# Forty mixer blocks with one 512-column product for the high weights, their halves added on eviction, and five modulation blocks placed earlier

## The chip, the core and the metric

The kernel runs on one core of one Trainium2 chip. The metric is the device time of one execution in microseconds (us). The core's engines run beside each other and meet through semaphores: TensorE (PE in the profile, with PEld for its weight loads), VectorE (DVE), ScalarE (ACT), GpSimd (POOL) and SyncE (SP), whose queue issues the large loads. Products land in PSUM; everything else lies in SBUF.

## What is computed

One decoder layer on 256 tokens of width 1024, in float32. The part that the change touches is the token mixer, and the condition vector that scales it:

```python
mod = jax.nn.silu(c) @ mod_w[l] + mod_b[l]
sh1, sc1, g1, sh2, sc2, g2 = jnp.split(mod, 6, axis=-1)
h = rmsnorm(x, norm1_g[l]) * (1.0 + sc1[:, None]) + sh1[:, None]
z = h @ w_in                      # q, k, v, g_dn, r, conv_b, conv_c, conv_h, gate_a, gate_c
...                               # chunked linear attention gives o
y_gla = o @ w_gla_out
conv_out = causal_short_conv(conv_c * conv_h, conv_w)
y_conv = (conv_b * conv_out) @ w_conv_out
y = jax.nn.sigmoid(gate_a) * y_gla + jax.nn.sigmoid(gate_c) * y_conv
x = x + g1[:, None] * (y @ w_out)
...                               # then a mixture of 64 experts and a final norm
```

## The kernel before

**Blocks.** The mixer's weights are 88 blocks of 128 x 1024 floats (512 KB). Blocks 0 to 15 alternate between v and q/k. Then come groups of eight blocks, each block 128 output features: c (16 to 23), r (24 to 31), h (32 to 39), b (40 to 47), a (48 to 55), g (56 to 63), A (64 to 71, `w_gla_out`), C (72 to 79, `w_conv_out`), O (80 to 87, `w_out`). A group's two halves are named c0 and c1, and so on; i counts the four blocks of a half.

**Split precision.** Each weight block is split into a high part (`split_h`, ACT, L340) and a low part (`split_l`, DVE, L347), both of type float32r, into one of three `sp` tiles that hold two blocks each. The activations are split in the same way. `mm_blk` (L356) does three products for each of eight k: high weights by high activations, high weights by low activations, low weights by high activations. All three are 128 x 128 weights by 256 columns and add up in one PSUM half bank.

**PSUM.** Two consecutive blocks, a pair, share one z bank of 512 floats. There are four z banks, taken in turn by `zt()`, so a bank is used again four pairs, that is eight blocks, later. The first product into a bank waits until the engine that read its last contents is done.

**The loop.** One pass for each block b writes, into the engines' in-order queues: the work marked "first", `split_h` of block b+5, the eviction of the block before (`evac`), the work marked "pre", `split_l` of block b+5, the other work due at b, and then block b's products. An eviction does nothing for the first block of a pair; for the second it works on 512 columns. For c it is an ACT copy (`c_evac`, L710), for h a DVE multiply (L763), for b a DVE multiply four blocks later (`b_evac`, L726), for A and C DVE multiplies and adds, for a and g an ACT sigmoid.

**Modulation.** The 48 blocks of `mod_w` come through the same ring of 12 load buffers as the weights. Each is one DVE multiply with a sum (`mod_blk`, L257). 16 are done beside blocks 0 to 15; the table `MODS` names the block beside which each of the other 32 is done. When `mod_blk` or `split_l` is done with a ring buffer, SP issues the next load into it.

**Other work that is named below.** The gates of the linear attention (L453, L463 and L464 on ACT, L449 to L456 on DVE); `k_evac` (L719, L720), the masks of the attention (L498, DVE) and the state products behind them (L506, PE); the reciprocal of the attention's norm (L549, DVE) and the products that spread it (`gla_ss4`, L556, PE, before block 39); `o_norm` (L561, L563); `conv_taps` (L587); the splits of the activations (`put_h` and `put_l`, one line each for all uses, L567 and L570). After the last C block, O0 takes `yhl`, whose last quarter is split just before; its products are written so that k 0 to 5 of two blocks come ahead of k 6 and 7. `st.free` gives a large buffer to the stream of expert weights: tile T9 at block 80 is one (L107). Behind the mixer come the router and 8 groups of experts, whose weights are loaded in 2 MB units.

Of the kernel before, what the change touches and what calls it, by code (L numbers as in the profile page):

```python
# [17 lines left out]
KT = 8  # L18
# [13 lines left out]
FAR = 8192.0  # L32
START = (2, 2, 0, 2, 8)
XS = 38
MODS = (16, 17, 18, 19, 22, 26, 27, 28, 31, 33, 34, 35, 37, 39, 41, 43, 45, 47, 49, 51, 52, 53, 54, 55, 56, 57, 58,
        59, 60, 61, 62, 63)
LA = 5
SPLIT = ("T6", "T7", "T3")
EPS = 1e-6
# [78 lines left out]
def trunk_kernel(ctx: ExitStack, tc: tile.TileContext, xT: bass.AP, c: bass.AP, modw: bass.AP,  # L118
# [4 lines left out]
    V, S, T, G = nc.vector, nc.scalar, nc.tensor, nc.gpsimd  # L123
# [11 lines left out]
    def mt(*shape):  # L135
        i = mring[rot["m"] % len(mring)]
        rot["m"] += 1
        return pm.tile([128, *(shape or (512,))], F32, name="m", tag=f"M{i}")

    def zt(*shape):  # L140
        i = rot["z"] % 4
        rot["z"] += 1
        return pz.tile([128, *(shape or (2, TOK))], F32, name="z", tag=f"Z{i}")
# [16 lines left out]
    mod_at = {}  # L160
    for n, b in enumerate(MODS):
        mod_at.setdefault(b, []).append((4 + n // 4, n % 4))
    blocks = []
    for j in range(len(items) + LA):
        if j < len(items):
            kind, n, i = items[j]
# [38 lines left out]
    gt2 = sm.tile([128, 1024], F32, name="gt")  # L205
# [62 lines left out]
    A1 = sm.tile([128, KT], F32, name="A1")  # L268
    hhl = big.tile([128, 2, KT, TOK], F32R, name="hhl", tag="T4")
    hl = (hhl[:, 0], hhl[:, 1])  # L270
# [23 lines left out]
    for i in range(2):  # L294
        ps = mt()
# [11 lines left out]
    ps = mt(2, 256)  # L307
    for k in (0, 1, 4, 5):
        if k % 4 == 0:
            start_warm(1 + k // 4)  # L310
        for tt in range(TT):
            T.matmul(ps[:, tt, 0:1], xnt[:, k, 128 * tt:128 * tt + 128], onec, start=(k == 0 and tt == 0),  # L312
                     stop=(k == 5), skip_group_check=True)
# [15 lines left out]
    def sp_slot(b):  # L329
        p = b // 2  # L330
        return p % 3 if p <= XS else (p - XS - 1) % 2

    def sp(b):
        return spt[sp_slot(b)][:, b % 2]

    def split_h(b):
        if b >= len(items):
            return
        kind, n, i = items[b]
        S.copy(sp(b)[:, 0], st.block("w", n, i))  # L340

    def split_l(b):
        if b >= len(items):
            return
        kind, n, i = items[b]
        t = sp(b)
        V.tensor_sub(t[:, 1], st.block("w", n, i), t[:, 0].bitcast(F32))  # L347
        st.bdone("w", n, i)
# [3 lines left out]
    def mm_blk(b, ps, rhs, k0=0, k1=KT, clear=True):  # L352
        t = sp(b).rearrange("p s (k m) -> p s k m", k=KT)
        for k in range(k0, k1):
            for n, (ws, rs) in enumerate(PASSES):
                T.matmul(ps, t[:, ws, k], rhs[rs][:, k], start=(clear and k == 0 and n == 0),  # L356
                         stop=(k == KT - 1 and n == 2), skip_group_check=True)

    def mm_qk(b, kk):
        t = sp(b).rearrange("p s (h m) -> p s h m", h=2 * H)  # L360
        for n, (ws, rs) in enumerate(PASSES):
            for h in range(2 * H):
                pb = (pq, pk)[h // H][h % H // 2]
                T.matmul(pb[:, h % 2], t[:, ws, h], hl[rs][:, kk],  # L364
                         start=(kk == 0 and h % 2 == 0 and n == 0),
                         stop=(kk == KT - 1 and h % 2 == 1 and n == 2), skip_group_check=True)

    def mm_v(b, kk, pv):
        t = sp(b)
        for n, (ws, rs) in enumerate(PASSES):  # L370
            for tt in range(TT):
                for hh in range(2):
                    T.matmul(pv[tt][hh], hl[rs][:, kk, 128 * tt:128 * tt + 128],  # L373
                             t[:, ws, 512 * hh:512 * hh + 512],
                             start=(kk == 0 and n == 0), stop=(kk == 7 and n == 2))

    def prep(b):

        k = b // 2
        split_h(b)  # L380
        if b % 2 == 0:
            if k > 0:
                mods(k)
            h_mod(k)
            if k > 0:
                split_l(b - 1)
                if k < KT - 1:
                    xnorm(k + 1)
            h_lo(k)
            split_l(b)  # L390
            if k == 0:
                S.copy(rstd1, pr1[:, :TOK])
                xnorm(1)
# [9 lines left out]
    L = {}  # L403
# [162 lines left out]
    def put_h(dst, x, s):  # L566
        S.copy(dst[:, 0, s], x)  # L567

    def put_l(dst, x, s):
        V.tensor_sub(dst[:, 1, s], x, dst[:, 0, s].bitcast(F32))  # L570
# [22 lines left out]
    def at(i, f, *a):  # L593
        todo.setdefault(i, []).append((f, a))
# [4 lines left out]
    def pre(i, f, *a):  # L599
        todo.setdefault((i, "pre"), []).append((f, a))  # L600
# [71 lines left out]
    def x1_out(k, ps):  # L672
        V.scalar_tensor_tensor(xres[:, k], ps, modc[:, 16 + k:17 + k], xres[:, k], op0=OP.mult, op1=OP.add)
# [31 lines left out]
    ps = None  # L705
# [37 lines left out]
    def r_evac(q, ps):  # L743
        S.activation(L["sr"][:, 2 * q:2 * q + 2], ps, AF.Silu)

    def evac(b, kind, n, i, ps):
        if kind in ("v", "qk"):
            return
        if n == "O1" and i >= 2:
            x1_out(4 + i, ps[i - 2][:, 0])  # L750
            at(b + 1, x1_stat, 4 + i)
            return
        half = int(n[1:])
        q = 2 * half + i // 2
        s = slice(2 * q, 2 * q + 2)
        if i % 2 == 0:
            return
        if kind == "r":
            pre(b, r_evac, q, ps)
        elif kind == "c":  # L760
            pre(b, c_evac, s, ps)
        elif kind == "h":
            V.tensor_mul(cu0[:, s], cu0[:, s], ps)  # L763
            at(b + 1, conv_tap0, s)
            at(b + 2, conv_taps, s)
        elif kind == "b":
            pre(b + 4, b_evac, q, ps)
            at(b + 5, b_high, q)
            at(b + 6, b_low, q)
        elif kind in "ag":  # L770
            if kind == "a" and q == 0:
                L["sg"] = big.tile([128, 2, KT, TOK], F32, name="sg", tag="T8")
            S.activation(L["sg"][:, 0 if kind == "a" else 1, s], ps, AF.Sigmoid)
        elif kind == "A":
            V.tensor_mul(L["sg"][:, 0, s], L["sg"][:, 0, s], ps)
            if q == 3:
                st.free("T11")
        elif kind == "C":
            if q == 0:
                L["yhl"] = big.tile([128, 2, KT, TOK], F32R, name="yhl", tag="T4")  # L780
            y, t = L["sg"][:, 0, s], L["sg"][:, 1, s]
            V.tensor_mul(t, t, ps)
            V.tensor_add(y, y, t)
            put_h(L["yhl"], y, s)
            if q < 3:
                at(b + 1, put_l, L["yhl"], y, s)
            else:
                put_l(L["yhl"], y, s)
                at(b, st.free, "T9")
                at(b + 2, o_setup)  # L790
        elif kind == "O":
            for k in range(2 * q, 2 * q + 2):
                x1_out(k, ps[:, k % 2])
            at(b + 1, x1_stats, q)
# [9 lines left out]
    def run(b):  # L804
        for f, a in todo.pop(b, []):
            f(*a)
# [8 lines left out]
            ahead.setdefault(b - (LA if b // 2 <= XS + 2 else LA - 2), []).append(b)  # L815
    for b, (kind, n, i) in enumerate(items):
        if i % 2 == 0 and kind not in ("v", "qk"):
            ps = (zt(), zt()) if n == "O1" and i == 2 else zt()
        nxts = ahead.get(b, ())
        early = b + LA < nb and items[b + LA][0] in ("v", "qk")  # L820
        run((b, "first"))
        if early:
            prep(b + LA)
        for nxt in nxts:
            if items[nxt - 1][0] == "qk":
                split_l(nxt - 1)
            split_h(nxt)
        if pend:
            evac(b, *pend)
        run((b, "pre"))  # L830
        for nxt in nxts:
            split_l(nxt)
        run(b)
        if kind == "v":
            mm_v(b, b // 2, pv)
        elif kind == "qk":
            mm_qk(b, b // 2)
        else:
            rhs = {"A": "ohl", "C": "chl", "O": "yhl"}.get(kind)
            rhs = hl if rhs is None else (L[rhs][:, 0], L[rhs][:, 1])  # L840
            if n == "O0" and i == 0:
                mm_blk(b, ps[:, 0], rhs, 0, 6)
                mm_blk(b + 1, ps[:, 1], rhs, 0, 6, clear=False)
                mm_blk(b, ps[:, 0], rhs, 6, 8)
            elif n == "O0" and i == 1:
                mm_blk(b, ps[:, 1], rhs, 6, 8)
            elif n == "O1" and i >= 2:
                mm_blk(b, ps[i - 2][:, 0], rhs)
            else:
                mm_blk(b, ps[:, i % 2], rhs)  # L850
        pend = (kind, n, i, ps)
        if b % 2 and all(sp_slot(a) != sp_slot(b) for a in range(b + 1, nb)):
            st.free(SPLIT[sp_slot(b)])
# [30 lines left out]
    O1, O2 = OO[:, :, 0], OO[:, :, 1]  # L884
# [264 lines left out]
    for g in range(NGRP):  # L1149
# [6 lines left out]
        ps = pa.tile([128, D], F32, name="a")  # L1156
# [21 lines left out]
        ps = pa.tile([128, D], F32, name="a")  # L1178
# [137 lines left out]
```

## Time and profile before

| | |
|---|---|
| time, median of 3 runs | 1210.06 us (1209.81 to 1211.35) |
| the profiled execution | 1211.79 us, span of its trace 1210.0 us |
| mean granted TensorE clock | 0.885; 1.00 in every 20 us stretch from 0 to 320 us |
| busy share: PE, PEld, DVE, ACT | 75%, 40%, 31%, 19% |
| HBM traffic | 477.84 MB, 394 GB/s over the span |

The times of the sections below are those of the profiled execution, in us from the start of its span. The busy shares are means over two very different parts: the mixer up to about 296 us, and the experts behind it. In the timeline rows, a row merges instructions of one line that follow each other, so its length is that of all of them, and the first number in brackets is the idle time of the engine ahead of it, with what ended it.

### The profile page before, as it was taken

The numbers are of one execution on the slowest core, as the hardware profiler recorded it, in microseconds if no ns is written. First come the engines' busy times: TensorE is split into PE (matmuls) and PEld (weight loads), VectorE is DVE, ScalarE is ACT, GpSimd is POOL, SyncE is SP. The second block draws the span as 40 slices with busy tenths as digits, with TensorE's granted clock in tenths as the row PEclk, the third lists the DMA queues.
The fourth block names the chain that finished last, engine by engine and source line by source line (L and its number), as shares of the span: only waits on it lengthen the run. The fifth ranks groups of instructions, "written<-read, shape, count | busy, mean of one in ns | idle before, by whom it ended". The sixth has DMA issues, their size and how long they took to land.

```text
span 1210.0 us, 14630 instructions
## 1 busy us (share of the span) xinstructions
PE 912.2 (75%) x6202; PEld 478.8 (40%) x6202; DVE 380.1 (31%) x718; ACT 224.7 (19%) x375; POOL 4.0 (0%) x15
## 2 busy tenths in 40 slices
PE   9999999999887667766666767565667666757565
PEld 6999999999341212121212122121212111312112
DVE  8967699654430202111111111020202000302103
ACT  6774545343310101010101010000000000100002
POOL 0000000000000000000000000000000000000000
PEclk9999999999997978788888788898878787988787
DMA  9997579979999999999999999999999999999995
GB/s 368 394 342 246 183 233 346 368 277 358 413 430 431 430 431 430 432 429 431 431 431 431 429 433 429 431 432 429 430 432 431 430 430 432 429 429 432 430 428 222
DMA packets 51482, 477.84 MB, mean 395 GB/s; under 512 B 5970, under 2 KB 6098, under 8 KB 27092
## 3 DMA queue, kind: packets, MB, share of 16 engines
q1 hardware_dynamic: 50544, 475.81, 95.2%
q8 instruction: 50, 0.82, 0.2%
q10 hardware_dynamic: 868, 1.05, 0.2%
q14 instruction: 20, 0.16, 0.0%
HBM read 475.79 MB, written 1.05 MB: 394 GB/s over the span
## 4 chain that ended last, share of the span: by engine, by line
DMA 67%; PE 29%; DVE 3%; ACT 0%; issue 0%; DVEq 0%; SPq 0%; ACTq 0%
DMA ring<-in_ew_dram 39%; DMA unit<-in_ew_dram 28%; PE z L356 17%; PE a L1043 3%; PE m L364 2%; PE z L373 2%; PE m L1015 1%; PE m L1070 1%; PE a L1195 1%; PE m L529 0%; PE z L220 0%; PE m L506 0%; PE m L525 0%; PE m L296 0%; PE m L312 0%
## 5 line engine op out<-in xcount | busy, mean ns | idle before, releaser
L1043 PE MATMUL a<-unit,xt 128*32 128x512 f32 x1408 | 202.0, 703 | 92.4 <-DMA unit<-in_ew_dram 92.4
L1043 PE MATMUL a<-unit,gt 128*32 128x512 f32 x672 | 113.1, 810 | 67.6 <-DMA unit<-in_ew_dram 66.2
L356 PE MATMUL z<-hhl,sp 128*128 128x256 f32 x1152 | 140.9, 284 | 0.0
L356 PEld LDWEIGHTS z<-hhl,sp 128*128 128x128 f32 x1152 | 138.9, 192 | 1.6 <-issue 1.5
L1043 PEld LDWEIGHTS a<-unit,xt 128*32 128x32 f32 x1408 | 42.3, 119 | 232.3 <-DMA unit<-in_ew_dram 129.2
L1043 PE MATMUL a<-ring,xt 128*32 128x512 f32 x624 | 92.3, 718 | 45.9 <-DMA ring<-in_ew_dram 45.9
L1019 ACT ACTIVATE xt<-m,modc,A 128x128 f32<-128x128 f32 x64 | 25.9, 454 | 527.4 <-PE m L1015 527.4
L347 DVE TENSOR_TENSOR sp<-ring,sp 128x1024 fp32r<-128x1024 f32 x88 | 106.9, 1221 | 42.0 <-ACT sp L340 41.9
L340 ACT CAST sp<-ring 128x1024 fp32r<-128x1024 f32 x88 | 91.5, 1049 | 94.9 <-PE z L356 64.7
L1074 DVE TENSOR_TENSOR wk<-wk,m 128x512 f32<-128x512 f32 (+2 forms) x64 | 41.8, 655 | 196.3 <-PE m L1070 196.3
L1061 DVE TENSOR_TENSOR xt<-a,xt 128x1024 f32<-128x1024 f32 (+3 forms) x19 | 20.0, 1055 | 263.2 <-PE a L1043 255.2
L1043 PEld LDWEIGHTS a<-unit,gt 128*32 128x32 f32 x672 | 22.0, 131 | 152.2 <-DMA unit<-in_ew_dram 104.0
L1070 PE MATMUL m<-xt,pwt 128*128 128x512 f32 (+2 forms) x136 | 63.8, 611 | 5.4 <-DVE xt L1061 5.4
L1043 PE MATMUL a<-ring,gt 128*32 128x512 f32 x288 | 51.0, 842 | 22.2 <-DMA ring<-in_ew_dram 20.0
L1015 PEld LDWEIGHTS m<-Pm,wk 128*128 128x128 f32 x512 | 58.7, 192 | 19.0 <-issue 18.7
L1043 PEld LDWEIGHTS a<-ring,xt 128*32 128x32 f32 x624 | 20.1, 123 | 115.3 <-DMA ring<-in_ew_dram 59.9
L1015 PE MATMUL m<-Pm,wk 128*128 128x128 f32 x512 | 62.4, 279 | 3.7 <-DVE Pm L1004 2.9
L1051 DVE TENSOR_TENSOR gt<-gt,a 128x512 f32<-128x512 f32 x16 | 11.0, 687 | 172.4 <-ACT gt L1050 172.4
L257 DVE SCALAR_TENSOR_TENSOR xt<-ring,xt 128x1024 f32<-128x1024 f32 x48 | 58.6, 1220 | 0.6 <-DMA ring<-in_modw_dram 0.3
L1021 DVE TENSOR_SCALAR xt<-m,A,modc 128x128 f32<-128x128 f32 x64 | 23.3, 406 | 103.0 <-PE m L1015 103.0
L1070 PEld LDWEIGHTS m<-xt,pwt 128*128 128x128 f32 x136 | 25.6, 203 | 50.2 <-issue 37.7
L1050 ACT ACTIVATE gt<-a 128x512 f32<-128x512 f32 x16 | 9.6, 597 | 180.9 <-PE a L1043 180.9
(251 smaller groups left out, 637.5 us busy)
## 6 DMA issues: line engine op xcount, KB each, us to landing
unit<-in_ew_dram SPq DMA_DIRECT2D x130, 2048.0 KB, 38.8
ring<-in_ew_dram SPq DMA_DIRECT2D x54, 2048.0 KB, 38.8
ring<-in_win_dram SPq DMA_DIRECT2D x88, 512.0 KB, 8.0
ring<-in_modw_dram SPq DMA_DIRECT2D x48, 512.0 KB, 6.8
ring<-in_ew_dram SPq DMA_DIRECT2D x12, 512.0 KB, 5.8
unit<-in_el_dram SPq DMA_DIRECT2D x4, 1024.0 KB, 31.6
unit<-in_el_dram SPq DMA_DIRECT2D x8, 512.0 KB, 14.8
xt<-in_xT_dram SPq DMA_DIRECT2D x2, 512.0 KB, 4.8
```

What stands on the lines that cost most here:

```text
L257: V.scalar_tensor_tensor(scr, st.block("m", i, b), 1.0, cB, op0=OP.mult, op1=OP.mult, accum_out=modc[:, 4 * i + b:4 * i + b + 1])
L340: S.copy(sp(b)[:, 0], st.block("w", n, i))
L347: V.tensor_sub(t[:, 1], st.block("w", n, i), t[:, 0].bitcast(F32))
L356: T.matmul(ps, t[:, ws, k], rhs[rs][:, k], start=(clear and k == 0 and n == 0), stop=(k == KT - 1 and n == 2), skip_group_check=True)
L364: T.matmul(pb[:, h % 2], t[:, ws, h], hl[rs][:, kk], start=(kk == 0 and h % 2 == 0 and n == 0), stop=(kk == KT - 1 and h % 2 == 1 and n == ...
L373: T.matmul(pv[tt][hh], hl[rs][:, kk, 128 * tt:128 * tt + 128], t[:, ws, 512 * hh:512 * hh + 512], start=(kk == 0 and n == 0), stop=(kk == ...
L1015: T.matmul(ps[j], acc[:, tt, f:f + 128], Pm[:, tt], start=(tt == 0), stop=(tt == 1))
L1019: S.activation(xg[:, k], ps[j], AF.Identity, bias=B2[:, k:k + 1], scale=A2[:, k:k + 1])
L1021: V.tensor_scalar(xg[:, k], ps[j], A2[:, k:k + 1], B2[:, k:k + 1], op0=OP.mult, op1=OP.add)
L1043: T.matmul(ps[32 * j:32 * j + 32, 512 * hh:512 * hh + 512], lhsT[:, 32 * j:32 * j + 32], w[:, j, 512 * hh:512 * hh + 512], start=first, st ...
L1070: T.matmul(ps[:, :w], pwt[:, tt], X["y"][:, s], start=True, stop=True)
L1074: V.tensor_add(total[:, tt, s], total[:, tt, s], ps[:, :w])
```

## The change

In 40 of the blocks (c1, h, g, A, C, the last two blocks of O0 and the first two of O1) the first two of the three products become one: the high weights meet both activation parts, 512 columns, and the result fills a whole bank. The low weights then add their 256 columns to the first half of it. So a pair takes two z banks, and each of the 40 blocks is followed by an ACT copy of its second half to `hsum` (a strip of `gt2`) and a DVE add of that to the first half; the second block's sum goes beside the first one's, and the old eviction follows. There is one `hsum`. In `MODS`, the modulation blocks that stood beside blocks 52, 54, 56, 58 and 61 now stand beside 36, 38, 40, 42 and 44, each later one moving up in the order.

```diff
-MODS = (16, 17, 18, 19, 22, 26, 27, 28, 31, 33, 34, 35, 37, 39, 41, 43, 45, 47, 49, 51, 52, 53, 54, 55, 56, 57, 58,
-        59, 60, 61, 62, 63)
+MODS = (16, 17, 18, 19, 22, 26, 27, 28, 31, 33, 34, 35, 36, 37, 38, 39, 40, 41, 42, 43, 44, 45, 47, 49, 51, 53, 55,
+        57, 59, 60, 62, 63)
...
+    def mm_wide(b, ps, rhs):
+
+        t = sp(b).rearrange("p s (k m) -> p s k m", k=KT)
+        for k in range(KT):
+            T.matmul(ps, t[:, 0, k], rhs[:, :, k], start=(k == 0), stop=False, skip_group_check=True)
+            T.matmul(ps[:, 0], t[:, 1, k], rhs[:, 0, k], start=False, stop=(k == KT - 1), skip_group_check=True)
...
+    hsum = gt2[:, 704:960]
+
+    def wide(n, i):
+        return n in ("h0", "h1", "g0", "g1", "A0", "A1", "C0", "C1", "c1") or (n, i // 2) in (("O0", 1), ("O1", 0))
+
     def evac(b, kind, n, i, ps):
         if kind in ("v", "qk"):
             return
+        if wide(n, i):
+            S.copy(hsum, ps[i % 2][:, 1])
+            V.tensor_add(ps[0][:, i % 2], ps[i % 2][:, 0], hsum)
+            ps = ps[0]
...
-            ps = (zt(), zt()) if n == "O1" and i == 2 else zt()
+            ps = (zt(), zt()) if n == "O1" and i == 2 or wide(n, i) else zt()
...
+            elif wide(n, i):
+                mm_wide(b, ps[i % 2], parts)
```

**ACT, around block 21.** Here z_775 is the bank of the pair 20/21 (c1's first), z_776 and z_822, z_823 are the further banks that the change takes, t9 and gb hold the attention's gates, and sp is a weight split. Before:

```order
L340 CAST sp_179<-ring_69 128x1024
L453 ACT_TABLE_LOAD
L453 ACTIVATE t9_181<-t9_181 128x1024
L340 CAST sp_179<-ring_69 128x1024
L710 COPY t8_126<-z_775 128x512
L463 ACTIVATE t9_181<-t9_181 128x1024
L464 ACTIVATE gb_182<-gb_182 128x1024
L340 CAST sp_180<-ring_69 128x1024 x2
```

And now:

```order
L340 CAST sp_179<-ring_69 128x1024
L762 COPY gt_77<-z_775 128x256
L460 ACT_TABLE_LOAD
L460 ACTIVATE t9_181<-t9_181 128x1024
L340 CAST sp_179<-ring_69 128x1024
L762 COPY gt_77<-z_776 128x256
L717 COPY t8_126<-z_775 128x512
L470 ACTIVATE t9_181<-t9_181 128x1024
L471 ACTIVATE gb_182<-gb_182 128x1024
L340 CAST sp_180<-ring_69 128x1024
L762 COPY gt_77<-z_822 128x256
L340 CAST sp_180<-ring_69 128x1024
```

The pair's copy (L710, now L717) stands behind a second copy, L762, and waits for the DVE add between the two.

**DVE, blocks 36 to 38.** Here z_1272 and z_1237 are the bank of the pair 34/35 before and now, z_1365 and z_1319 that of 36/37, and scr2 holds the attention's norm. Before:

```order
L763 TENSOR_TENSOR t8_126<-t8_126,z_1272 128x512
L347 TENSOR_TENSOR sp_180<-ring_69,sp_180 128x1024
L587 SCALAR_TENSOR_TENSOR gb_182<-t8_126,colt_75,gb_182 128x255
L587 SCALAR_TENSOR_TENSOR gb_182<-t8_126,colt_75,gb_182 128x254
L587 SCALAR_TENSOR_TENSOR gb_182<-t8_126,colt_75,gb_182 128x255
L587 SCALAR_TENSOR_TENSOR gb_182<-t8_126,colt_75,gb_182 128x254
L347 TENSOR_TENSOR sp_178<-ring_69,sp_178 128x1024
L257 SCALAR_TENSOR_TENSOR xt_70,modc_124<-ring_69,xt_70 128x1024
L763 TENSOR_TENSOR t8_126<-t8_126,z_1365 128x512
L549 RECIPROCAL scr2_123<-scr2_123 128x256
```

And now, from behind the first split and with the four taps left out of the middle:

```order
L347 TENSOR_TENSOR sp_180<-ring_69,sp_180 128x1024
L257 SCALAR_TENSOR_TENSOR xt_70,modc_124<-ring_69,xt_70 128x1024
...
L763 TENSOR_TENSOR z_1319<-z_1319,gt_77 128x256
L347 TENSOR_TENSOR sp_178<-ring_69,sp_178 128x1024
L257 SCALAR_TENSOR_TENSOR xt_70,modc_124<-ring_69,xt_70 128x1024
L763 TENSOR_TENSOR z_1319<-z_1320,gt_77 128x256
L779 TENSOR_TENSOR t8_126<-t8_126,z_1319 128x512
L556 RECIPROCAL scr2_123<-scr2_123 128x256
```

One more modulation block (L257) and two adds (now L763) stand ahead of the reciprocal.

**DVE, blocks 44 to 46.** Here z_1510 and z_1447 are the bank of the pair 40/41 (b0's first) before and now. Before:

```order
L347 TENSOR_TENSOR sp_178<-ring_69,sp_178 128x1024
L561 TENSOR_TENSOR gb_182<-gb_182,m_1479 128x512
L563 SCALAR_TENSOR_TENSOR gb_182<-gb_182,colt_75,t9_181 128x256 x2
L347 TENSOR_TENSOR sp_179<-ring_69,sp_179 128x1024
L570 TENSOR_TENSOR ohl_1581<-gb_182,ohl_1581 128x512
L257 SCALAR_TENSOR_TENSOR xt_70,modc_124<-ring_69,xt_70 128x1024
L726 TENSOR_TENSOR gb_182<-gb_182,z_1510 128x512
```

And now:

```order
L347 TENSOR_TENSOR sp_178<-ring_69,sp_178 128x1024
L568 TENSOR_TENSOR gb_182<-gb_182,m_1423 128x512
L570 SCALAR_TENSOR_TENSOR gb_182<-gb_182,colt_75,t9_181 128x256 x2
L257 SCALAR_TENSOR_TENSOR xt_70,modc_124<-ring_69,xt_70 128x1024
L347 TENSOR_TENSOR sp_179<-ring_69,sp_179 128x1024
L577 TENSOR_TENSOR ohl_1522<-gb_182,ohl_1522 128x512
L257 SCALAR_TENSOR_TENSOR xt_70,modc_124<-ring_69,xt_70 128x1024
L733 TENSOR_TENSOR gb_182<-gb_182,z_1447 128x512
```

The modulation block of 44 has come in ahead of the multiply that clears the bank of 40/41.

## Rows read from the trace of the kernel before

**Rows 1.** The page, the chain that ended last: share of the span by engine.
```profile
DMA 67%; PE 29%; DVE 3%; ACT 0%; issue 0%; DVEq 0%; SPq 0%; ACTq 0%
```
**Rows 2.** The same chain in order of time: start us, us, what.
```profile
20.65 2.75 PE z L373 x12
23.39 2.87 PE m L364 x24
...
149.88 100.79 PE z L356 x840
...
367.50 31.81 DMA unit<-in_ew_dram
```
**Rows 3.** Windows: length, busy PE, PEld, DVE, ACT, POOL, clock, DMA share, GB/s.
```profile
139.00:173.00 34.00, 33.94 (x279) 33.56 (x276) 32.47 (x51) 16.42 (x23) 0.00 (x0) 1.00 0.71 226
270.00:275.00 5.00, 5.00 (x44) 5.00 (x43) 2.96 (x4) 1.63 (x3) 0.00 (x0) 1.00 0.44 156
```
**Rows 4.** Timeline: start us, us, engine line; an ACT copy and DVE tensor-tensor, 256 columns.
```profile
61.05 0.37 ACT L424 COPY e<-z 128x256 f32<-128x256 f32 x1 [0.94 <-PE z L420]
...
12.27 0.42 DVE L276 TENSOR_TENSOR t<-xt,m 128x256 f32<-128x256 f32 x1 [0.78 <-PE m L321]
```
**Rows 5.** Timeline, 83 to 106 us: ACT, then DVE, then PE.
```profile
83.13 1.28 ACT L453 ACT_TABLE_LOAD   x1 [3.44 <-DVE t L450]
...
85.39 1.03 ACT L340 CAST sp<-ring 128x1024 fp32r<-128x1024 f32 x1
86.32 0.58 ACT L710 COPY t<-z 128x512 f32<-128x512 f32 x1
86.80 1.06 ACT L463 ACTIVATE t<-t 128x1024 f32<-128x1024 f32 x1
...
89.78 1.23 DVE L347 TENSOR_TENSOR sp<-ring,sp 128x1024 fp32r<-128x1024 f32 x1 [0.95 <-ACT sp L340]
...
103.90 1.34 DVE L498 COPY_PREDICATED gc<-cmask,m 128x512 f32<-128x512 int32 x2
...
94.40 1.04 PE L481 MATMUL m<-ident,gb 128*128 128x128 f32 x8
...
104.68 1.99 PE L506 MATMUL m<-t,gc 64*128 64x256 f32 x14 [1.09 <-DVE gc L498]
```
**Rows 6.** Timeline, 138 to 181 us: DVE, then PE.
```profile
138.63 0.68 DVE L763 TENSOR_TENSOR t<-t,z 128x512 f32<-128x512 f32 x1
...
143.13 1.23 DVE L347 TENSOR_TENSOR sp<-ring,sp 128x1024 fp32r<-128x1024 f32 x1 [0.86 <-ACT sp L340]
...
153.79 1.23 DVE L347 TENSOR_TENSOR sp<-ring,sp 128x1024 fp32r<-128x1024 f32 x1 [0.25 <-ACT sp L340]
...
172.53 1.22 DVE L257 SCALAR_TENSOR_TENSOR xt<-ring,xt 128x1024 f32<-128x1024 f32 x1
...
173.68 0.69 DVE L726 TENSOR_TENSOR gb<-gb,z 128x512 f32<-128x512 f32 x1
...
179.81 0.68 DVE L726 TENSOR_TENSOR gb<-gb,z 128x512 f32<-128x512 f32 x1
...
147.91 1.97 PE L556 MATMUL m<-scr,P 128*128 128x256 f32 x8
149.52 50.74 PE L356 MATMUL z<-hhl,sp 128*128 128x256 f32 x420
```
**Rows 7.** Timeline, 269 to 275 us: ACT, then DVE, then PE, then SP.
```profile
269.68 1.05 ACT L340 CAST sp<-ring 128x1024 fp32r<-128x1024 f32 x1 [1.83 <-PE z L356]
...
271.85 0.69 DVE L570 TENSOR_TENSOR yhl<-sg,yhl 128x512 fp32r<-128x512 f32 x1 [0.69 <-ACT yhl L567]
272.46 1.22 DVE L347 TENSOR_TENSOR sp<-ring,sp 128x1024 fp32r<-128x1024 f32 x1
...
269.56 2.92 PE L356 MATMUL z<-yhl,sp 128*128 128x256 f32 x23
...
274.17 0.38 SPq L107 DMA_DIRECT2D unit<-in_ew_dram  x1
```

More of the change, by code (lines that the diff above doesn't have):

```diff
@@ L838, in trunk_kernel @@
         else:
-            rhs = {"A": "ohl", "C": "chl", "O": "yhl"}.get(kind)
-            rhs = hl if rhs is None else (L[rhs][:, 0], L[rhs][:, 1])
+            parts = L[{"A": "ohl", "C": "chl", "O": "yhl"}[kind]] if kind in "ACO" else hhl
+            rhs = parts[:, 0], parts[:, 1]
             if n == "O0" and i == 0:
```

## The prediction, made before the changed kernel ran

> **What bounds the kernel now.** I read the chain that ended last first. As shares [rows 1] it is two thirds DMA and under a third TensorE. In order of time [rows 2] the two parts do not mix: up to 367.50 us the chain runs along TensorE, with 840 mixer products (35 blocks) back to back from 149.88; from there on it is expert loads alone. So a microsecond gained or lost by TensorE in the mixer moves the release of every buffer that the expert stream waits for, and comes out at the end one to one. Second, what a product costs: 100.79 us over 840 is 120 ns for 256 columns, a block of 24 is 2.88 us [rows 2]. Third, who stands close behind TensorE. From 139 to 173 us VectorE is busy 32.47 of 34.00 us [rows 3], and where it hands over the margin is small: the state products wait 1.09 us for its masks at 104.68 [rows 5], and the multiply that clears the bank of the pair 40/41 ends at 173.68 + 0.69 = 174.37 [rows 6], while block 48, which needs that bank, starts nine blocks after block 39, at 149.52 + 9 x 2.88 = 175.4. In this stretch VectorE has about 1.1 us to spare. The reader is to see that the share of 31% for VectorE on the page says nothing about it.
>
> **The wide product.** Columns do not change: 3 x 256 before, 512 + 256 now. One product and one weight load of three per k go. The v blocks already run 512 columns with a load each: 12 in 2.75 us, 229 ns; their neighbours run 256 columns, 24 in 2.87 us, 120 ns [rows 2]. So a k takes 229 + 120 = 349 ns for 359, 10 ns less; a block of eight k saves 0.08 us, 40 blocks 3.2 us. Bounds: nothing, or, if the fixed part of every product went, 768 columns at one a cycle: the granted clock is 1.00 [rows 3], the level of 2.4 GHz, so 320 ns and 0.31 us a block. I take 0.08, since both forms stand in rows of this program with a load ahead of each product.
>
> The 512-column row shows 229 ns. The Trainium skill (TensorE: Matmul & The Clock Gate, Back-to-back issue gap) gives about 131 ns for a 512-column product in a sustained stream with loads. By that a k would take 251 ns, and 28 blocks would give back some 22 us more than I count; the row speaks against it.
>
> **The evictions.** Each wide block adds an ACT copy of 256 columns, 0.37 us, and a DVE add, 0.42 us by the nearest row, which reads PSUM but does not write it [rows 4] (bounds: 0.37, the copy of the same size, and 0.69, the multiply of 512 columns [rows 6]). ACT's 15 us lie beside TensorE (16.42 busy of 34.00 [rows 3]). They cost where somebody waits for the hand-over of ACT to DVE and back, or for DVE. Wide pairs that follow each other use a bank again after four blocks, so an eviction has two blocks, 5.6 us; split, copy, add and multiply take 1.05 + 0.37 + 0.42 + 0.69 = 2.5 us behind the second block. In g, A and C this is hidden; in g five modulation blocks leave (5 x 1.15) where eight adds come (8 x 0.42).
>
> **First place, c1 into r0: +2.0 us.** Four wide blocks take the z banks twice as fast, so block 24 now needs the bank of the pair 20/21, which was block 28's. Three blocks ahead of 94.40 [rows 5], block 24 starts at 85.76; with 4 x 0.08 saved, 85.4. But the eviction of 20/21 stands in ACT's queue behind the gates: ACT sits idle until 83.13 for the scan on DVE, then table load, exponential, split; the pair's copy starts at 86.32 [rows 5]. Now the copy of block 21 comes first (86.7), then the add (87.1), then the pair's copy (87.7). Block 24 starts 2.0 late. DVE says the same: its own queue has the add of block 22 ahead of the split at 89.78, and that add waits for an ACT copy that now comes at about 91.0, so the split starts at 91.4, 1.6 late; one more add makes 2.0, and the masks at 103.90 and the state products at 104.68 move by it [rows 5]. The two waits overlap: 2.0 once.
>
> **Second place, h1 into a0: +6.0 us.** From the multiply at 138.63 to the one at 173.68 VectorE is all but continuous; its idle time is 0.86 and 0.25 us [rows 6]. The table puts the modulation blocks of 36, 38, 40, 42 and 44 in here, each 1.15 us (172.53 to 173.68 [rows 6]): 5.75. Four adds (blocks 36 to 39), 0.40 each when they follow others: 1.6. The first multiply moves back by copy and add, between 0 and 0.8; I take 0.6. Together 7.95, less 1.1 idle: 6.85. The bank of 40/41 comes free at 174.37 + 6.85 = 181.2, block 48 is ready at 175.4 or a little before: +5.8. Block 50 waits for the multiply of 179.81, which ends at 180.49 + 6.85 = 187.3, against 181.2 + 5.76 = 187.0: +0.3, less rounding, 6.0 in all. On the way the reciprocal, on which L556 at 147.91 waits, is also late, by some 1.6; that is part of the 6.0, since VectorE's queue sets the end of this stretch either way. What TensorE saves in c1 and h (12 blocks) is lost in these two waits. Loads move with the table: five 512 KB loads go earlier on SP's queue. DMA share is 0.71 here [rows 3], so I cost them at nothing; with a share near 1 each would take 1.3 us of the stream (0.52 MB at the page's mean of 394 GB/s).
>
> **Third place, C1 into O0: +0.8 us.** The last quarter of `yhl` now waits for split, copy and add. Split ends at 270.73, copy 271.1, add 271.5, then multiply, add, `put_h`, `put_l` as before: `put_l` ends at about 274.4 instead of 272.54. TensorE wants it for k 6, 37 products after 269.56, at 274.0 [rows 7]: 0.4. In O, two evictions hand x1 to transposes two blocks later; between 0 and 0.8, I take 0.4.
>
> **The sum.** 2.0 + 6.0 + 0.8 - 28 x 0.08 (g, A, C, O: 2.2) = 6.6 us more. The profiled execution, 1211.79, becomes 1218.4; it lies 1.7 above the median of its runs, so 1216.7 us.
>
> **Rivals.** (a) Faster. VectorE has room after all, and only the products count: 1210.06 - 3.2 = 1206.9. It decides at block 48's bank: if the work added ahead of that multiply is below 1.1 idle + 1.1 margin = 2.2 us, nothing waits there. I count 7.95 before idle, so the counts would have to be wrong by a factor of three, and c1's wait would have to vanish too. For it: 1.5 of the 34 us are idle, and the wait for ACT is a hand-over that DVE may fill with other work. Against: its queue is in order, and the idle time that the rows show there is in the 2.2 already. 7%.
> (b) The products are faster than their rows: TensorE's loads hide wholly behind 512 columns and a k takes 320 ns. Then the 28 blocks give 8.7 instead of 2.2, and the time is 1210.2: no change. For it: a 256-column product and its load are equally long, so either could set the 120 ns. Against: the 512-column rows have the same fixed part. With half of it, 1213.5. 12%. At the far end a 512-column product would take no longer than the 120 ns of a 256-column one [rows 2], and a k 240: 28 x 8 x 119 ns = 26.7 in place of 2.2, 1192. The rows at 229 leave it 1%. The page named above, with its 131 ns, would make that 1195.
> (c) The expert stream loses more than TensorE. SP gives T9's buffer away only behind the split at 272.46, and DMA is short of work there (0.44 [rows 3]; the load at 274.17 [rows 7]). Split and load come 1.9 later than TensorE's own shift: 1216.7 + 1.9 - 0.4 = 1218.2, if nothing downstream absorbs it. 25%, within slower.
> (d) The change does not do what it says: the program's order shows the wide products, copies and adds in place, so I give this nothing.
>
> **How the numbers follow.** Forecast and (c) together 80%, near it to both sides, (b) 12%, (a) 7%, the far end 1%. 0.2% is 2.4 us, about what a measurement of this kernel can tell from no change. Slower by more than that (above 1212.5): 79%; within it, with most of (b): 12%; faster, with (a), the far end and the lowest part of (b): 9%. The range leaves out (a) and the whole of (b): low 1211.5 (three quarters of (b)'s effect); high, with (c) and adds at 0.69 ahead of block 48 (4 x 0.29 = 1.2): 1219.5.
>
> **What would show it.** In the trace of the changed kernel: a mean step of about 349 ns per k in g, A and C (320 would show (b)); an idle stretch of TensorE ahead of block 24, released by the ACT copy of 20/21; one ahead of L556, released by the reciprocal; one of 3 to 6 us ahead of block 48, released by `b_evac`; VectorE without idle time from 139 to 190; none ahead of blocks 60, 68 and 76; the chain passing to DMA some 6 us after 367.50. I am wrong if blocks 48 and 50 start without a wait, or if the chain's change to DMA has not moved while TensorE is late.

## The result and the profile after

The changed kernel takes 1219.95 us (median of 4 runs, 1218.11 to 1221.98) against 1210.62 for the kernel before (4 runs, 1209.81 to 1211.35): ratio 1.0075, 95% interval 1.0063 to 1.0087. Slower, as forecast, but by 9.3 us (7.6 to 10.5 by the interval) where 6.6 were worked out, and 0.45 us above the top of the range.

The page of the changed kernel, the chain that ended last, shares of the span [rows 1 is the same line of before]:

```profile
DMA 70%; PE 22%; DVE 5%; issue 1%; ACT 1%; DVEq 0%; SPq 0%; ACTq 0%
```

All waits of TensorE in the changed kernel from 60 to 300 us (engine, line, what it waited for: us in total, times, longest):

```profile
PE z L356 <- DVE gb L733: 4.1, 1, 4.1
PE m L563 <- DVE scr L556: 2.3, 1, 2.3
PE z L356 <- ACT t L717: 2.1, 1, 2.1
PE z L356 <- DVE yhl L577: 0.2, 1, 0.2
```

Before there was one, 1.1 us for the masks ([rows 5], at 104.68). It is gone, and the four places of the prediction stand in its stead: the copy of 20/21 ahead of block 24, the reciprocal ahead of block 39, `b_evac` ahead of block 48, `yhl` in O0. The stages through VectorE and ScalarE raise their part of the chain from 3 to 6%. TensorE's falls from 29 to 22%, since the chain takes other branches in places and leaves TensorE earlier (see the signs below), so these shares do not price the loss.

TensorE's timeline in the changed kernel at the first three, with the state products between them (start us, us, engine, line, operation, tiles, count, idle before and releaser):

```profile
87.59 10.38 PE L356 MATMUL z<-hhl,sp 128*128 128x256 f32 x72 [2.12 <-ACT t L717]
...
106.30 2.00 PE L513 MATMUL m<-t,gc 64*128 64x256 f32 x16
...
151.31 1.99 PE L563 MATMUL m<-scr,P 128*128 128x256 f32 x8 [2.29 <-DVE scr L556]
...
183.24 7.03 PE L356 MATMUL z<-hhl,sp 128*128 128x256 f32 x40 [4.13 <-DVE gb L733]
```

The row at 87.59 holds what the prediction left out. 72 products at 120 ns are 8.6 us; it takes 10.38. The row at 183.24 has 40 products in 7.03 us, where 40 x 120 ns are 4.8. Windows of the changed kernel behind the two waits, and two stretches with rows in before (a:b, us, busy time and count of PE, PEld, DVE, ACT, POOL, then granted clock, DMA share, GB/s):

```profile
88.90:92.20 3.30, 3.30 (x18) 3.30 (x17) 1.81 (x5) 2.96 (x5) 0.00 (x0) 0.50 0.84 257
92.30:96.00 3.70, 3.70 (x33) 3.70 (x32) 3.70 (x7) 2.11 (x3) 0.00 (x0) 1.00 0.56 185
139.00:173.00 34.00, 31.71 (x233) 28.92 (x233) 33.47 (x58) 17.15 (x25) 0.00 (x0) 1.00 0.76 232
183.30:187.80 4.50, 4.50 (x21) 4.50 (x22) 4.46 (x7) 2.02 (x3) 0.00 (x0) 0.50 0.84 282
188.00:191.00 3.00, 3.00 (x28) 3.00 (x27) 3.00 (x6) 1.57 (x2) 0.00 (x0) 1.00 0.75 255
```

From 183.30 to 187.80 TensorE is busy all the time and gets 21 products through, 214 ns each: the granted clock is 0.50, the level of 1.2 GHz. From 188 on it is 1.00 again, 28 in 3.00 us. In the trace of before the clock is 1.00 through the whole mixer, as in [rows 3], so a price for it had no row there. VectorE, 32.47 us busy from 139 to 173 before [rows 3], is now busy 33.47, 58 operations: it is full, as forecast.

Counted off block by block in the two timelines, and against block 16 (which starts 0.24 us earlier than before, for reasons that lie ahead of the change), TensorE is late by

| at block | late, us | what came in between |
|---|---|---|
| 24 | 2.1 | the wait for the copy of 20/21 |
| 25 | 3.5 | block 24 at half clock for most of its length, 4.11 us for 2.76 from the start of its first product to that of its last |
| 29 | 1.9 | the state products no longer wait for their masks (row at 106.30, without a wait): 1.9 us from their start to that of block 29, for 3.7 before |
| 38 | 1.5 | wide blocks save 0.4 |
| 39 | 3.7 | the wait for the reciprocal |
| 48 | 7.9 | the wait for `b_evac` |
| 49 | 9.9 | block 48 at half clock, 4.84 us for 2.76, counted in the same way |
| 80 | 8.3 | 24 wide blocks save 1.6 |
| 82 | 8.75 | the wait for `yhl` |
| 87 | 8.55 | |

From there it reaches the end one to one: counting bytes moved in the two traces, the stream is 8.5 to 8.7 us late at every point from 106 MB (340 us) to 465 MB (1175 us), and TensorE, in the same two traces without the 0.24, 8.3 at block 87. The spans differ by less (1210.0 and 1216.3): from 465 MB to its end the profiled execution of before took 44.3 us, that of the changed kernel 41.9. The prediction had set 1.7 us aside for this, by which the first of these executions lies above the median of its kernel.

### The profile page after: what moved, and what is told of

The parts are those of the page before. It is cut to its first block, busy times and chain, and to the rows that moved or that the text cites. A ratio compares the mean times of both kernels' runs of the same rounds, so it can differ in the third digit from the quotient of the medians.

```text
span 1216.3 us, 14066 instructions
## 1 busy us (share of the span) xinstructions
PE 899.1 (74%) x5882; PEld 464.0 (38%) x5882; DVE 394.1 (32%) x758; ACT 235.9 (19%) x415; POOL 3.9 (0%) x15
## 4 chain that ended last, share of the span: by engine, by line
DMA 70%; PE 22%; DVE 5%; issue 1%; ACT 1%; DVEq 0%; SPq 0%; ACTq 0%
DMA unit<-in_ew_dram 44%; DMA ring<-in_ew_dram 22%; PE z L356 6%; PE z L363 5%; DMA unit<-in_el_dram 2%; PE z L364 2%; PE a L1061 2%; PE m L371 2%; PE z L380 2%; DVE sp L347 1%; DMA ring<-in_win_dram 1%; DVE xt L257 1%; PE m L1033 1%; DMA ring<-in_modw_dram 1%; PE z L220 0%
## 5 line engine op out<-in xcount | busy, mean ns | idle before, releaser
L1061 PE MATMUL a<-unit,xt 128*32 128x512 f32 x1408 | 204.8, 712 | 96.4 <-DMA unit<-in_ew_dram 96.4
L1061 PE MATMUL a<-unit,gt 128*32 128x512 f32 x672 | 104.5, 754 | 65.0 <-DMA unit<-in_ew_dram 62.9
L1061 PE MATMUL a<-ring,xt 128*32 128x512 f32 x624 | 84.1, 660 | 46.3 <-DMA ring<-in_ew_dram 46.3
L356 PE MATMUL z<-hhl,sp 128*128 128x256 f32 x672 | 86.3, 291 | 6.2 <-DVE gb L733 4.1
L356 PEld LDWEIGHTS z<-hhl,sp 128*128 128x128 f32 x672 | 84.7, 199 | 7.9 <-issue 5.4
L257 DVE SCALAR_TENSOR_TENSOR xt<-ring,xt 128x1024 f32<-128x1024 f32 x48 | 58.5, 1219 | 0.3
L363 PE MATMUL z<-hhl,sp 128*128 128x512 f32 x160 | 57.1, 401 | 0.0
L364 PE MATMUL z<-hhl,sp 128*128 128x256 f32 x160 | 44.9, 280 | 0.0
```

What stands on the lines that cost most here:

```text
L257: V.scalar_tensor_tensor(scr, st.block("m", i, b), 1.0, cB, op0=OP.mult, op1=OP.mult, accum_out=modc[:, 4 * i + b:4 * i + b + 1])
L363: T.matmul(ps, t[:, 0, k], rhs[:, :, k], start=(k == 0), stop=False, skip_group_check=True)
L364: T.matmul(ps[:, 0], t[:, 1, k], rhs[:, 0, k], start=False, stop=(k == KT - 1), skip_group_check=True)
L1061: T.matmul(ps[32 * j:32 * j + 32, 512 * hh:512 * hh + 512], lhsT[:, 32 * j:32 * j + 32], w[:, j, 512 * hh:512 * hh + 512], start=first, st ...
```

## The experiments

Three theories stand. **A**: each place costs what stands in VectorE's or ScalarE's queue ahead of the release; five modulation blocks moved into 36 to 44 make the wait at block 48, and TensorE's clock falls because it stands still there. **B**: the hand-over of each wide pair costs, wherever the modulation is. **C**: the slow block behind the wait is contention, not the clock's answer to standing still. Lateness is again against block 16.

**wide_old_table.** The changed kernel with the old table.

```diff
-MODS = (16, 17, 18, 19, 22, 26, 27, 28, 31, 33, 34, 35, 36, 37, 38, 39, 40, 41, 42, 43, 44, 45, 47, 49, 51, 53, 55,
-        57, 59, 60, 62, 63)
+MODS = (16, 17, 18, 19, 22, 26, 27, 28, 31, 33, 34, 35, 37, 39, 41, 43, 45, 47, 49, 51, 52, 53, 54, 55, 56, 57, 58,
+        59, 60, 61, 62, 63)
```

> The changed kernel with the modulation table of the kernel before: only the wide products, copies and adds are left. Theory A (five modulation blocks moved into 36 to 44 fill VectorE and make the wait at block 48): the first place stays, block 24 waits about 2 us and TensorE runs at half clock for one block behind it, +1.6 us at block 29; at block 48 VectorE has 4 adds x 0.40 + 0.6 more and 2.2 us of room, so a wait of 0 to 0.5 us and no fall of the clock; 28 blocks give back 1.9, yhl costs 0.4: about 1210.3 us (1209.5 to 1212). Theory B (the hand-over of each wide pair, copy and add, makes the loss wherever it stands, the table does not matter): block 48 still waits over 3 us, 1216 to 1219 us.

Measured: 1212.08 against 1211.28, ratio 1.0009 (0.9999 to 1.0018). TensorE's waits from 60 to 300 us:

```profile
PE z L356 <- ACT t L717: 2.1, 1, 2.1
PE m L563 <- DVE scr L556: 1.3, 1, 1.3
PE m L513 <- DVE gc L505: 0.7, 1, 0.7
PE z L356 <- DVE yhl L577: 0.2, 1, 0.2
```

The wait of 4.1 us is gone, so the table made it, and B falls as the account of that wait. Some 0.6 us stay at 48 and 50 together. TensorE is 1.8 us late at block 87, and the time lies just above the range that was expected. Two things differ from the expectation. It left out block 39, where the wait for the reciprocal, 1.3 us, still costs 1.24: so much of B holds, h's copies and adds cost something with the old table too. And the same wait of 2.1 us at block 24 is not followed by a fall of the clock here. Window of this kernel behind it:

```profile
88.50:92.00 3.50, 3.47 (x29) 3.47 (x30) 2.00 (x5) 3.50 (x5) 0.00 (x0) 1.00 0.50 133
```

**table_only.** The kernel before with the new table, by the same lines the other way round.

```diff
-MODS = (16, 17, 18, 19, 22, 26, 27, 28, 31, 33, 34, 35, 37, 39, 41, 43, 45, 47, 49, 51, 52, 53, 54, 55, 56, 57, 58,
-        59, 60, 61, 62, 63)
+MODS = (16, 17, 18, 19, 22, 26, 27, 28, 31, 33, 34, 35, 36, 37, 38, 39, 40, 41, 42, 43, 44, 45, 47, 49, 51, 53, 55,
+        57, 59, 60, 62, 63)
```

> The kernel before with the new modulation table alone, no wide product. Theory A: VectorE has 5 x 1.15 = 5.75 us more ahead of block 48 and 2.2 us of room, so block 48 waits 3.5 us, released by b_evac, and the block behind the wait runs at half clock, +2.1: 1215.7 us. If the wait comes but the clock does not fall behind it, 1213.6. Theory B: the moved blocks are hidden, 1210 to 1211 us.

Measured: 1215.93 against 1211.28, ratio 1.0034 (1.0023 to 1.0045). TensorE's timeline, then the window behind the wait:

```profile
180.18 20.08 PE L356 MATMUL z<-hhl,sp 128*128 128x256 f32 x153 [3.15 <-DVE gb L726]
```

```profile
180.20:183.50 3.30, 3.30 (x16) 3.30 (x17) 3.26 (x5) 0.79 (x2) 0.00 (x0) 0.54 0.81 264
```

The wait is 3.15 us for 3.5 worked out, block 48 then takes 4.32 us, TensorE is 5.1 late in all. By the trace the table alone, with not one wide product, makes 5.1 of the 8.55 us; the time is up by 4.1 (2.8 to 5.5), of the changed kernel's 9.3. In the traces the two halves of the change are worth 1.8 and 5.1, together 6.9; in one kernel they cost 8.55. Of the 1.65 between, 1.55 stands in the waits at 39 and 48 and 0.5 in the clock behind 48, less 0.4 lost in wide_old_table at blocks 50 and 51 and not in the changed kernel. That VectorE's 2.2 us of room can be used up only once fits the waits; no run tries it alone.

**no_c1.** The changed kernel with c1 narrow.

```diff
-        return n in ("h0", "h1", "g0", "g1", "A0", "A1", "C0", "C1", "c1") or (n, i // 2) in (("O0", 1), ("O1", 0))
+        return n in ("h0", "h1", "g0", "g1", "A0", "A1", "C0", "C1") or (n, i // 2) in (("O0", 1), ("O1", 0))
```

> The changed kernel with c1 narrow again (blocks 20 to 23), the new table kept. Theory A: no wait ahead of block 24 and no fall of the clock there, so block 29 is 0.2 early instead of 1.6 late; the second place starts from a multiply that moves with TensorE and keeps its whole loss; four blocks lose 0.06 each: 1220.0 - 1.9 + 0.2 = 1218.3 us. Rival: VectorE's queue sets block 48 whatever c1 does, then the wait there grows by what c1 gives and the time stays at 1219.5 to 1220.

Measured: 1218.86 against 1211.28, ratio 1.0055 (1.0038 to 1.0072), which does not part the two numbers. The trace says more. TensorE's waits, and the windows behind the waits at 39 and 48:

```profile
PE z L356 <- DVE gb L733: 3.5, 1, 3.5
PE m L563 <- DVE scr L556: 2.3, 1, 2.3
PE m L513 <- DVE gc L505: 1.1, 1, 1.1
PE z L356 <- DVE yhl L577: 0.2, 1, 0.2
```

```profile
151.70:155.50 3.80, 3.80 (x17) 3.24 (x16) 3.73 (x7) 0.00 (x0) 0.00 (x0) 0.69 0.75 238
182.40:188.00 5.60, 5.60 (x26) 5.60 (x27) 5.56 (x9) 2.40 (x4) 0.00 (x0) 0.50 0.88 301
```

The wait at 24 is gone, and 1.9 us with it at block 29. But at block 39 the same wait of 2.3 us as in the changed kernel is now followed by a lower clock: the products that spread the reciprocal take 0.5 us longer and block 39 takes 1.1 more, so that TensorE is only 0.2 better at block 40. Block 48's wait is 0.7 shorter, and the clock behind it costs 2.62 in place of 2.07: TensorE ends 8.2 late, only 0.35 better. The multiply that clears the bank of 40/41 moves by 0.9 with the 1.9 and not by all of it, since VectorE now stands still once, for ScalarE's copy of block 39, which comes behind a split that waits for TensorE's slow block:

```profile
157.15 0.43 DVE L763 TENSOR_TENSOR z<-z,gt 128x256 f32<-128x256 f32 x1 [0.89 <-ACT gt L762]
```

The reciprocal, ahead of that, moves by the whole 1.9, as A says. What c1 costs is real where it stands; in this execution the clock behind later waits took most of the gain back.

**busy_wait48.** The changed kernel; TensorE works through the wait.

```diff
+        if b == 48:
+            warm48 = mt(4, 128)
+            rot["m"] -= 1
+            for _ in range(18):
+                T.matmul(warm48, onesb, onesb[:, None, :].to_broadcast([128, 4, 128]), start=True, stop=True)
```

> The changed kernel with 18 idle products (512 bf16 columns of ones into a free bank, nobody reads them, about 0.22 us each) in TensorE's queue ahead of block 48, so that it works through the wait for b_evac. Theory A (the granted clock falls since TensorE stands still): no stretch at 0.5 behind block 48, which takes 2.8 us instead of 4.84: 1217.9 us. Rival C (the slow block is contention for operands with VectorE, ScalarE or the loads, idle or not): block 48 still takes 4.8 us, 1220 us. If the products run longer than the wait, up to 1 us of the gain is lost.

Measured: 1218.05 against 1211.28, ratio 1.0056 (1.0040 to 1.0073); on the same chip as the three above. TensorE's timeline, and the window behind the wait:

```profile
178.79 4.06 PE L854 MATMUL m<-onesb 128*128 128x512 bf16 x18
183.01 9.24 PE L356 MATMUL z<-hhl,sp 128*128 128x256 f32 x72 [0.17 <-DVE gb L733]
```

```profile
183.10:187.00 3.90, 3.90 (x33) 3.90 (x34) 3.87 (x6) 1.45 (x2) 0.00 (x0) 1.00 0.89 314
```

Block 48 starts where it did (183.01 for 183.24) with the same work on VectorE and a DMA share of 0.89 beside it, at clock 1.00, and takes 2.83 us instead of 4.84. C falls: the 2.07 us are the clock's, and it fell since TensorE stood still. This is what the sum lacked. Not all of it is won: 0.4 is lost again at blocks 49 to 51, where the slow block had covered the wait for the bank of 42/43, and TensorE ends 6.9 late for 8.55, 1.65 better.

**no_c1_old_table.** The changed kernel with c1 narrow and the old table, both edits at once: wide in h, g, A, C and O.

```diff
-        return n in ("h0", "h1", "g0", "g1", "A0", "A1", "C0", "C1", "c1") or (n, i // 2) in (("O0", 1), ("O1", 0))
+        return n in ("h0", "h1", "g0", "g1", "A0", "A1", "C0", "C1") or (n, i // 2) in (("O0", 1), ("O1", 0))
-MODS = (16, 17, 18, 19, 22, 26, 27, 28, 31, 33, 34, 35, 36, 37, 38, 39, 40, 41, 42, 43, 44, 45, 47, 49, 51, 53, 55,
-        57, 59, 60, 62, 63)
+MODS = (16, 17, 18, 19, 22, 26, 27, 28, 31, 33, 34, 35, 37, 39, 41, 43, 45, 47, 49, 51, 52, 53, 54, 55, 56, 57, 58,
+        59, 60, 61, 62, 63)
```

> Old table, c1 narrow: wide products in h, g, A, C and O. Theory A (each place has its own wait): no wait ahead of block 24; h's adds and copies still make block 39 wait for the reciprocal (1.2 us in wide_old_table) and blocks 48 and 50 for 0.4 together; 36 blocks give back 2.1, yhl costs 0.4: about 0.1 us under the kernel before, between -1 and +1. Rival (the two places are coupled by VectorE, whose queue sets block 48): what c1 gives is lost again at 39 and 48, +1 to +2 us.

Measured: 1209.87 against 1210.88, ratio 0.9995 (0.9986 to 1.0004). TensorE is 0.04 late at the end: 1.24 lost at block 39, 0.6 at 48 and 50, 0.4 at 82, the rest saved. Against wide_old_table TensorE ends 1.74 better, which is what c1 lost there: with the old table the two places are not coupled.

**wide_tail** and **wide_tail_C1.** Old table (put back as in wide_old_table), wide from block 56 on; the last line is the second kernel's, without the last pair of C1.

```diff
-        return n in ("h0", "h1", "g0", "g1", "A0", "A1", "C0", "C1", "c1") or (n, i // 2) in (("O0", 1), ("O1", 0))
+        return n in ("g0", "g1", "A0", "A1", "C0", "C1") or (n, i // 2) in (("O0", 1), ("O1", 0))
...
+        return n in ("g0", "g1", "A0", "A1", "C0") or (n, i // 2) == ("C1", 0) or (n, i // 2) in (("O0", 1), ("O1", 0))
```

> Old table, wide products in g, A, C and O alone (28 blocks from 56 on). Theory A: the first two places are gone, TensorE starts block 56 as before, 24 blocks give 1.6 us and four more 0.2, the wait for yhl costs 0.4: 1.4 us under the kernel before, ratio 0.9988. If the load for T9 behind the later split counts in full, 1.5 us less of gain: no difference.

> As wide_tail, but the last two blocks of C1 (78 and 79) narrow again. Theory A: the wait for yhl at block 82 (0.41 us) goes and 2 x 0.11 us are lost: 0.2 us faster than wide_tail. If the load for T9 that waits for the last split matters at the end, the stream of expert loads is up to 1.5 us earlier than in wide_tail; theory A says 0.35 at most, which is how much later it was than TensorE in the changed kernel.

Measured: 1209.19 and 1209.27 against 1210.88, ratios 0.9982 (0.9973 to 0.9991) and 0.9987 (0.9978 to 0.9996). TensorE ends 1.37 and 1.57 us early, as worked out to a tenth; the times do not part the two. In the traces the stream is 0.3 us earlier against TensorE in the second, so the load for T9 behind the last split is worth about that, not 1.5.

**wide_late.** c1 narrow, three modulation blocks moved behind everything that waits.

```diff
-        return n in ("h0", "h1", "g0", "g1", "A0", "A1", "C0", "C1", "c1") or (n, i // 2) in (("O0", 1), ("O1", 0))
+        return n in ("h0", "h1", "g0", "g1", "A0", "A1", "C0", "C1") or (n, i // 2) in (("O0", 1), ("O1", 0))
-MODS = (16, 17, 18, 19, 22, 26, 27, 28, 31, 33, 34, 35, 36, 37, 38, 39, 40, 41, 42, 43, 44, 45, 47, 49, 51, 53, 55,
-        57, 59, 60, 62, 63)
+MODS = (16, 17, 18, 19, 22, 26, 27, 28, 31, 33, 34, 35, 43, 45, 47, 49, 51, 52, 53, 54, 55, 56, 57, 58, 59, 60, 61, 62, 63, 64, 65, 66)
```

> c1 narrow, wide products in h, g, A, C and O, and the table of the kernel before with the modulation blocks of 37, 39 and 41 moved to 64, 65 and 66. Theory A (VectorE's room between 139 and 174 decides): 3 x 1.15 = 3.45 us leave where 4 adds of 0.40 and 0.6 of hand-over come, so blocks 48 and 50 start without a wait and the wait for the reciprocal at 39 is under 0.5; 36 blocks give back 2.1, yhl costs 0.4: 1.5 to 1.7 us under the kernel before, ratio 0.9987. Rival (the hand-over itself, not VectorE's load, delays the reciprocal): block 39 waits 1.2 us as in wide_old_table, ratio 0.9997.

Measured: 1209.04 against 1210.88, ratio 0.9986 (0.9977 to 0.9995). The time is theory A's, but the trace says otherwise on block 39: blocks 48 and 50 start without a wait, while the reciprocal still holds TensorE up (1.24 us later than before, as in the two kernels with more work on VectorE). VectorE's timeline, lines one lower than in the changed kernel:

```profile
144.21 1.22 DVE L346 TENSOR_TENSOR sp<-ring,sp 128x1024 fp32r<-128x1024 f32 x1
146.66 0.43 DVE L762 TENSOR_TENSOR z<-z,gt 128x256 f32<-128x256 f32 x1 [1.23 <-ACT gt L761]
147.13 0.69 DVE L778 TENSOR_TENSOR t<-t,z 128x512 f32<-128x512 f32 x1
147.73 1.75 DVE L555 RECIPROCAL scr<-scr 128x256 f32<-128x256 f32 x1
```

ScalarE's, same kernel:

```profile
145.31 1.05 ACT L339 CAST sp<-ring 128x1024 fp32r<-128x1024 f32 x1 [0.70 <-PE z L362]
146.26 0.36 ACT L761 COPY gt<-z 128x256 f32<-128x256 f32 x1
```

VectorE stands idle for 1.23 us: its add waits for a copy that stands behind a weight split on ScalarE, and the reciprocal, which needs neither, waits behind the add. Here it is order, not load. TensorE ends 0.6 us early by the trace, at the edge of what the times say, 1.7 (0.6 to 2.8); the time's match with theory A's number does not bear the theory out.

**wide_best.** The answer to that: wide_late with the reciprocal ahead of the eviction, and C1's last pair narrow.

```diff
-    pre(38, gla_ss3)
+    first(38, gla_ss3)
-        return n in ("h0", "h1", "g0", "g1", "A0", "A1", "C0", "C1") or (n, i // 2) in (("O0", 1), ("O1", 0))
+        return n in ("h0", "h1", "g0", "g1", "A0", "A1", "C0") or (n, i // 2) in (("C1", 0), ("O0", 1), ("O1", 0))
```

> wide_late with two edits: the reciprocal (gla_ss3) stands ahead of the eviction of block 37 in VectorE's queue instead of behind it, and the last two blocks of C1 are narrow. Theory: in wide_late VectorE stands still for 1.23 us until the copy of block 37, which stands behind a weight split in ScalarE's queue, and the reciprocal waits behind it; ahead of it the reciprocal ends by 147.3 us, so TensorE has no wait at block 39 (1.24 in wide_late), none at 82 (0.41): block 87 starts 2.0 us earlier against block 16 than in the kernel before, ratio 0.9980 to 0.9985. Rival: the load on VectorE makes the wait, which then moves to the tap or the split behind the reciprocal, and block 48 waits instead; ratio 0.9990 to 1.0.

Measured: 1207.35 against 1211.21, ratio 0.9966 (0.9952 to 0.9979): faster than both kernels, and by more than was expected. VectorE's timeline, then all waits of TensorE from 60 to 300 us:

```profile
145.36 1.75 DVE L555 RECIPROCAL scr<-scr 128x256 f32<-128x256 f32 x1
147.02 0.40 DVE L762 TENSOR_TENSOR z<-z,gt 128x256 f32<-128x256 f32 x1
```

```profile
PE m L512 <- DVE gc L504: 1.1, 1, 1.1
```

The reciprocal fills the gap and starts 2.4 us earlier, the add behind it finds its copy done, and the only wait left is the one that the kernel before has. TensorE ends 2.4 us early, for 2.0 worked out: block 39 starts 0.35 earlier against block 38 than in the kernel before. The time is 4.1 us down (2.5 to 5.8); what goes beyond 2.4 no trace here accounts for.

## Why the prediction was right and wrong

| step | predicted | trace | |
|---|---|---|---|
| first place, c1 into r0 | +2.0 | +1.9 at block 29 | right |
| second place, h1 into a0, with what c1 and h save | +6.0 | +8.1 | short by the clock |
| third place, `yhl` | +0.4 | +0.4 | right |
| third place, x1 in O | +0.4 | 0 | the lower bound |
| 28 blocks saved | -2.2 | -1.8 | too much |
| sum | +6.6 | +8.55 | |

**The step that failed is the second place**, and in it the silent assumption that TensorE comes out of a wait as it went in. The waits themselves came as worked out: the reciprocal is late by 2.2 (1.6 was said), `b_evac`'s bank by 4.3 more, 6.5 together, less the 0.5 that h saves: 6.0 at block 48. Then block 48 runs at 1.2 GHz, +2.07. busy_wait48 shows it alone: same wait, same neighbours, TensorE kept at work, 2.0 us off in the trace at block 49 and 1.65 at the end, where it is 6.9 late, for 6.6 forecast. In the time it is 1.0056 of the kernel before for 1.0075, about 2.3 us, with intervals that overlap: the trace shows the gain, the times alone do not. Without these 2.07 the sum is 0.1 us from the trace; so close is luck, since the smaller misses of the table (0.1, 0.4, 0.4) cancel. The range had a term for adds of 0.69 us and one for the load of T9, none for the clock; 2.07 less, the time would lie inside it.

**The first place** went by its rows. The copies and the add come in the order that was read, the pair's copy from 86.95 to 87.54 (87.1 to 87.7 was said, and this execution runs 0.24 early). ScalarE in the changed kernel:

```profile
86.09 0.36 ACT L762 COPY gt<-z 128x256 f32<-128x256 f32 x1
86.95 0.59 ACT L717 COPY t<-z 128x512 f32<-128x512 f32 x1 [0.50 <-DVE z L763]
```

The clock fell here too, 1.45 us, which the prediction did not have either. It cost nothing in the end: at block 29 the state products had waited for masks anyway [rows 5], and their 1.8 of lateness on VectorE (105.46 for 103.90, against block 16) sets it: in wide_old_table, without the fall, block 29 is as late. A loss ahead of another wait costs only what sticks out of it.

**The second place's release** went by its rows too. VectorE's multiply in the changed kernel:

```profile
182.41 0.68 DVE L733 TENSOR_TENSOR gb<-gb,z 128x512 f32<-128x512 f32 x1
```

It started at 173.68 before [rows 6], 8.7 later now (9.0 against block 16); 2.0 from the first place and 6.85 for VectorE's own work make 8.85. table_only shows the load alone, 3.15 us of wait where 5.75 less 2.2 were to be expected. The reason that was given for the reciprocal, VectorE's load, is only part of it. In wide_late, with less load, 1.24 us of lateness stay at block 39, and there they are a place in the queue; in the changed kernel VectorE works all the time ahead of it, so no run parts load from place there. The +0.3 at block 50 did not show in the changed kernel, where the slow block 48 covers it; in busy_wait48 it is there.

**The saving** is 0.055 us a block in g and A and 0.11 in most of C, for 0.08. TensorE's timeline in the changed kernel, a g block and a C block:

```profile
212.94 0.40 PE L363 MATMUL z<-hhl,sp 128*128 128x512 f32 x1
213.18 0.28 PE L364 MATMUL z<-hhl,sp 128*128 128x256 f32 x1
213.30 0.40 PE L363 MATMUL z<-hhl,sp 128*128 128x512 f32 x1
...
266.91 0.39 PE L363 MATMUL z<-chl,sp 128*128 128x512 f32 x1
267.14 0.28 PE L364 MATMUL z<-chl,sp 128*128 128x256 f32 x1
267.26 0.39 PE L363 MATMUL z<-chl,sp 128*128 128x512 f32 x1
```

From one wide product to the next it is 0.35 to 0.36 us; over eight k it comes to 353 and 347 ns, for 360 before. Rival (b), 320, is out. So is the figure of 131 ns that the Trainium skill (TensorE: Matmul & The Clock Gate, Back-to-back issue gap) gives for 512 columns: here they take 0.23 to 0.24 us, and the 18 bf16 products of busy_wait48, each with a load too, start 0.216 us apart.

**The other rivals.** (a) fell with the first wait. (c) was right in its cause and small in its effect. The load for T9, at 274.17 before [rows 7], is in the changed kernel's SP queue

```profile
283.97 0.38 SPq L107 DMA_DIRECT2D unit<-in_ew_dram  x1
```

9.8 us later, 1.3 more than TensorE; but from 340 us on the stream is only some 0.3 us later than TensorE (8.6 for 8.3, both against the trace of before as it stands), so what follows absorbs the rest.

**Signs.** The waits at 24, L556's and 48, VectorE without idle time, and no wait at 60, 68 and 76 all came, though of the five modulation blocks that move only three stood in g (56, 58 and 61), not five. The range's lower end, by its own words three quarters of (b)'s effect, would be 1211.8. The sign on the chain was badly chosen: it passes to DMA at 354.14, not some 6 us after 367.50 [rows 2], since it takes another branch through the experts; the count of bytes moved is the measure that holds.

## What to carry to other kernels

When a change makes TensorE wait, price the wait and the products behind it: behind waits of 3.15 to 4.13 us the next block ran at half clock for most of its length in all three traces that have such a wait in the mixer, and dummy products in the gap won 2.07 us at that block, 1.65 at the end. Before moving work into a stretch, count what its in-order queue can still take there, not its share of the page, and put work that waits for nobody ahead of work that waits. And a table that was balanced for one form of the code is part of that form: with the table kept and the wide product used only where evictions have room (wide_tail), the same idea is a gain, if only of 0.1 to 0.2%.

## What was not expected of the hardware

The length of a wait alone does not tell whether the clock falls. A wait of 2.1 us at block 24 was followed by clock 0.50 in the changed kernel and in busy_wait48 (window below), and by 1.00 in wide_old_table.

```profile
88.40:91.60 3.20, 3.20 (x17) 3.20 (x17) 1.71 (x4) 3.20 (x5) 0.00 (x0) 0.50 0.75 198
```

One of 2.3 us at block 39 was followed by clock 1.00 in the changed kernel and in busy_wait48, and by 0.69 on the mean in no_c1; the waits of 3.15, 3.45 and 4.13 us at block 48 (table_only, no_c1, the changed kernel) were all followed by a fall. What decides at 2.1 and 2.3 us was not tried. Up to block 35 the changed kernel, busy_wait48 and wide_old_table are one program, so executions of one kernel can differ in it. The spread of the times does not show this: the changed kernel's four runs spread over 3.9 us, but 33 runs of the kernel before, whose trace has no fall in the mixer, spread over 4.5.
